# The start of a two-layer decoder trunk: two projections of the first layer made block by block, or together along the rows of the weights

## The chip, the core and the metric

The kernel runs on one core of a Trainium2 chip, as one launch. The metric is the device time of that launch in microseconds (us); a smaller time is better. In the views of the profile the engines are called PE (matrix multiply), PEld (its weight load), DVE (vector engine), ACT (scalar engine), POOL and SP. SP issues most of the DMAs here.

## What is computed

The reference is a decoder trunk of two layers on 256 tokens of width 1024, float32 throughout. Each layer has three token mixers side by side on one normalised input, and then a squared-ReLU MLP:

```python
def hybrid_mixer(h, w_in, ...):
    p = h @ w_in
    (cq, ckv, k_rope, mq, mk, mv, rq, rk, rv, rg, g_mla, g_moba, g_ret) = jnp.split(p, IN_SPLIT_IDX, axis=-1)
    o_mla = mla_branch(cq, ckv, k_rope, mla_q_norm, mla_kv_norm, mla_w_q_up, mla_w_kv_up, cos_mla, sin_mla)
    o_moba = moba_branch(mq, mk, mv, cos_moba, sin_moba)
    o_ret = retention_branch(rq, rk, rv, rg, ret_gn_w, ret_gn_b, cos_ret, sin_ret)
    merged = (jax.nn.sigmoid(g_mla) * (o_mla @ w_branch_mla)
              + jax.nn.sigmoid(g_moba) * (o_moba @ w_branch_moba)
              + jax.nn.sigmoid(g_ret) * (o_ret @ w_branch_ret))
    return merged @ w_out

for l in range(DEPTH):
    h = rms_norm(x, attn_norm[l])
    x = x + hybrid_mixer(h, w_in[l], ...)
    h = rms_norm(x, mlp_norm[l])
    x = x + squared_relu_mlp(h, w_mlp_up[l], w_mlp_down[l])
return rms_norm(x, final_norm)
```

The columns of `w_in` that matter here come first: 416 columns for the MLA branch (256 for the query's low rank, 128 for the key's and value's, 32 for the shared rotary key), then three times 512 for the MoBA branch's `mq`, `mk` and `mv`. In the MLA branch the 416 columns are normalised again, then widened by `mla_w_q_up` and `mla_w_kv_up` to queries, keys and values of 8 heads.

## The kernel before

**Numbers in two parts.** Every operand of a large product is split into a high part (`hi`, written by ACT in a shorter format) and the rest (`lo`, by DVE: raw minus high). A product is then three matmuls into the same bank (`three`, lines 209 to 212): high by high, high by low, low by high. `fetch` (line 181) does the split for weights: L190 on ACT writes `whi`, L191 on DVE writes `wlo`. `split` (L225 on ACT, L226 on DVE) does it for activations, with the norm's gain. The norm's own factor, one number per token, is applied when a product is copied out of its bank.

**Weights.** `weight_plan` lays all weights out in the order of use, one DMA per load. A load mostly holds two row tiles (128 rows each) of 512 columns, 512 KB. `load_w` fetches in that order, one load ahead of use, except for the very first block. There are 4 buffers for raw weights and 6 each for `whi` and `wlo`.

**The first block, called "b0".** It multiplies x by the 416 MLA columns. In layer 0 it comes in five loads: the row tiles 0 and 1 singly, then three pairs. After it comes the block "mq" (512 columns, four loads of two row tiles), then "mk", both made by `project` (line 316): for each row tile k of x, for each of the two token halves, `three`. All row tiles of one block are done before the next block begins. x itself comes in parts: the row tiles 0 and 1 singly, then 2 and 3, then 4 to 7. x once more by tokens (`xrow`, for the norm's sum of squares) and the constants `K` are asked for after the first seven weight loads and before the rest.

**Banks.** There are eight accumulation banks, four in a group "acc" and four in a group "misc". `b0`, `mq`, `mk` and `mv` take two of "acc" each; transposes, scores and small products take "misc". In `kvup` (line 632) the MLA keys and then the values (into `vml`, L639) also take "acc".

**Order.** The code is a list of units (`prog`) with steps hung on them (`at`). A planner reorders the instructions of all engines by its own forecast of their times, except inside `manual_schedule` regions, where the written order stands. Such a region covers ACT, DVE and PE during the first block of layer 0 (`first_x`, line 1008). On the chip each engine then works strictly through its own list. The steps that matter here: `c_norms` (L543 to L558), which copies the 416 columns out of their banks and normalises them, hangs on unit 1 of "mq"; `c_turn` (L591 to L601), which transposes them and splits them into `cTh` and `cTl`, hangs on unit 1 of "mk"; `qrope`, `qnope` and `kvup` widen them between the units of "mv"; then the attention heads begin (scores `ps_s`, L666). Before x arrives PE multiplies zeros eight times (`warm`, L507, the constant `WARM`).

Of the kernel before, what the change touches and what calls it, by code (L numbers as in the profile page):

```python
# [7 lines left out]
F32 = mybir.dt.float32  # L8
# [5 lines left out]
P = 128  # L14
D = 1024
S = 256
NT = S // P
# [25 lines left out]
C_KV = [P * h + o + i for o in (0, NOPE) for h in range(MLA_H) for i in range(64)]  # L43


def b0_units(l):


    return ((0, 1), (1, 1), (2, 2), (4, 2), (6, 2)) if l == 0 else ((0, 2), (2, 2), (4, 2), (6, 2))


def weight_plan():

    plan = []

    def block(key, name, kt, cols, per):
        for j in range(0, kt, per):
            plan.append(((*key, j // per), name, (j, per), cols))

    def span(c, n):  # L60
        return range(c, c + n)

    for l in range(L):
        for i, unit in enumerate(b0_units(l)):
            plan.append(((l, "b0", i), "w_in", unit, C_MLA))
        block((l, "mq"), "w_in", KD, C_MQ, 2)
        block((l, "mk"), "w_in", KD, C_MK, 2)
        block((l, "mv"), "w_in", KD, C_MV, 2)
        mv, plan = plan[-4:], plan[:-4]
        for i, (key, name, kt, cols) in enumerate(  # L70
            (("qrope", "mla_w_q_up", 2, C_QROPE), ("qnope", "mla_w_q_up", 2, C_QNOPE), ("kvup", "mla_w_kv_up", 1, C_KV))
        ):
            block((l, key), name, kt, cols, kt)
            plan.append(mv[i])
        plan.append(mv[3])
        for i in range(2):
            block((l, "gmla%d" % i), "w_in", KD, span(C_GMLA + 512 * i, 512), 2)
        for i in range(2):
            block((l, "gmoba%d" % i), "w_in", KD, span(C_GMOBA + 512 * i, 512), 2)
        for i in range(2):  # L80
            block((l, "bmla%d" % i), "w_branch_mla", 4, span(512 * i, 512), 2)
        block((l, "rqk"), "w_in", KD, C_RQK, 2)
        block((l, "rv"), "w_in", KD, C_RV, 2)
        for n in range(4):
            block((l, "rg", n), "w_in", KD, span(C_RG + P * n, P), KD)
        for i in range(2):
            block((l, "bmoba%d" % i), "w_branch_moba", 4, span(512 * i, 512), 2)
        for i in range(2):
            block((l, "gret%d" % i), "w_in", KD, span(C_GRET + 512 * i, 512), 2)
        for i in range(2):  # L90
            block((l, "bret%d" % i), "w_branch_ret", 4, span(512 * i, 512), 2)
        for n in range(KD):
            block((l, "wout", n), "w_out", KD, span(P * n, P), KD)
        for f in range(NF + LAG):
            if f < NF:
                block((l, "up", f), "w_mlp_up", KD, span(P * f, P), KD)
            if f >= LAG:
                plan.append(((l, "down", f - LAG, 0), "w_mlp_down", (f - LAG, 1), range(D)))
    at, offset = {}, 0
    for key, name, (j, n), cols in plan:  # L100
        at[key] = (offset, n, len(cols))
        offset += P * n * len(cols)
    return plan, at, offset
# [22 lines left out]
def trunk(ctx: ExitStack, tc: tile.TileContext, x, wts, consts, gains, gfin, xtok, out):  # L126
# [36 lines left out]

    def load_w(*key):

        ahead = 0 if key[:2] == (0, "b0") else AHEAD
        while order and len(loaded) < ahead + 1:
            first = order.pop(0)
            loaded[first] = fetch(first)
        return loaded.pop(key)  # L170
# [10 lines left out]
    def fetch(key):  # L181
        offset, n, c = where[key]
        sz = n * c
        raw = started.pop(key, None)
        if raw is None:
            raw = wp.tile([P, 1024], F32, name="raw", bufs=4)
            transfer(key, raw)
        hi = wp.tile([P, 1024], F32R, name="whi", bufs=6)
        lo = wp.tile([P, 1024], F32R, name="wlo", bufs=6)
        nc.scalar.activation(hi[:, :sz], raw[:, :sz], AF.Copy)  # L190
        nc.vector.tensor_sub(lo[:, :sz], raw[:, :sz], hi[:, :sz].bitcast(F32))  # L191
        return (
            hi[:, :sz].rearrange("p (k c) -> p k c", k=n),
            lo[:, :sz].rearrange("p (k c) -> p k c", k=n),
        )
# [120 lines left out]
    def project(l, key, xn, n, done=None, before=None, turns=(range(NT),)):  # L316

        accs, ws = [], []
        units = b0_units(l) if key == "b0" else [(j, 2) for j in range(0, KD, 2)]
        count = len(units)  # L320

        def unit(i, ts, j):
            if not accs:
                accs.extend(acc_tile() for _ in range(NT))
            if before:
                before(i)
            if len(ws) <= j:
                ws.append(load_w(l, key, j))
            wh, wl = ws[j]
            for kk in range(units[j][1]):  # L330
                k = units[j][0] + kk
                ah, al = xn.k(k)
                for t in ts:
                    sl = slice(P * t, P * t + P)
                    three(accs[t][:, :n], ah[:, sl], al[:, sl], wh[:, kk, :], wl[:, kk, :], k == 0, k == KD - 1)
            if i == count * len(turns) - 1:
                done(accs)

        for turn, ts in enumerate(turns):
            for j in range(count):  # L340
                i = turn * count + j
                prog.append(((key, i), lambda i=i, ts=ts, j=j: unit(i, ts, j)))
# [168 lines left out]
    def at(slot, step):  # L511
        steps.setdefault(slot, []).append(step)

    def slot(key, j):
        return [k for k, _ in prog].index((key, j))
# [9 lines left out]
    def layer(l, xn, before):  # L525
# [5 lines left out]

        def c_norms():
            accs = b0
            if l == 0:
                xn.stats_rows(xrows)
            else:
                for n in range(KD):
                    xn.square(n)
                xn.stats()
# [17 lines left out]
                    dst = krx[t][:, 64 * (1 - i) : 64 * (1 - i) + 64].rearrange("p (two n) -> p two n", two=2)  # L557
                    nc.vector.tensor_copy(dst[:, :, 16 * i : 16 * i + 16], kr[:, 0, :, :])  # L558

        project(l, "b0", xn, 416, b0.extend, before, ((0,), (1,)) if l else (range(NT),))  # L560


        def moba_done(key):
            def done(accs):
                dst = mqkv[key] = [w2k(key) for _ in range(NT)]
                for t in range(NT):
                    nc.scalar.activation(dst[t], accs[t], AF.Copy, scale=xn.col[t])
                    if key != "mv":
                        xv = dst[t].rearrange("p (h d) -> p h d", h=MB_H)[:, :, 0:16]
                        rope(xv.rearrange("p h (two n) -> p h two n", two=2), K_COS_MB, K_SIN_MB, t, 8, MB_H)  # L570

            return done

        project(l, "mq", xn, 512, moba_done("mq"))
        at(slot("mq", 1), c_norms)
        at(slot("mq", 2), xn.stats_row)
        project(l, "mk", xn, 512, moba_done("mk"))


# [20 lines left out]
            nc.vector.tensor_copy(KK[0:64, 1::2, :], krT[0:64, None, :].to_broadcast([64, 4, S]))  # L600
            nc.vector.tensor_copy(KK[64:P, 0::2, :], krT[64:P, None, :].to_broadcast([64, 4, S]))  # L601

        at(slot("mk", 1), c_turn)

        def nope(dst, w, ks, copy):
            for b in range(2):
# [25 lines left out]
        def kvup():  # L632
            wh, wl = load_w(l, "kvup", 0)
            nope(mla["K"], (wh[:, :, 0:512], wl[:, :, 0:512]), (2,), nc.vector.tensor_copy)
            for t in range(NT):
                acc = acc_tile()
                sl = slice(P * t, P * t + P)
                three(acc, c["h"][:, 2, sl], c["l"][:, 2, sl], wh[:, 0, 512:1024], wl[:, 0, 512:1024], True, True)
                nc.scalar.activation(mla["v"][t], acc, AF.Copy)  # L639
# [348 lines left out]
    xn = Normed(G_ATT)  # L988
    xrows = [w2k("xrow") for _ in range(2 * NT)]
    nc.sync.dma_start(chunk(0), x[:, 0, :])  # L990
    for i, (k, n) in enumerate(b0_units(0)):
        if k == 2:
            nc.sync.dma_start(X[0][:, 2:4, :], x[:, 2:4, :])
        elif k == 4:
            nc.sync.dma_start(X[1], x[:, 4:8, :])
        tag, bufs = ("t4", T4) if n == 2 else ("w2k", W2K)
        started[0, "b0", i] = sb.tile([P, 512 * n], F32, name="raw0", tag=tag, bufs=bufs)
        transfer((0, "b0", i), started[0, "b0", i])
    for i in range(2):
        started[0, "mq", i] = wp.tile([P, 1024], F32, name="raw", bufs=4)  # L1000
        transfer((0, "mq", i), started[0, "mq", i])
    for q in range(2 * NT):
        nc.sync.dma_start(xrows[q], xtok[:, q // 2, 512 * (q % 2) : 512 * (q % 2) + 512])
    nc.sync.dma_start(K, consts[:, :K_DEC])

    started_order = ExitStack()

    def first_x(i):
        if i == 0:
            started_order.enter_context(  # L1010
                tc.manual_schedule(engines={mybir.EngineType.Activation, mybir.EngineType.DVE, mybir.EngineType.PE})
            )
            at(slot("b0", len(b0_units(0)) - 1), started_order.close)
        k, n = b0_units(0)[i]
        for j in range(k, k + n):
            xn.take(j, False)

    before = first_x
    for l in range(L):
# [1 line left out]


W2K = 17
WARM = 8
ENDS = 4
FIRST = 3
WHOLE = 1
# [1 line left out]
T4 = 9  # L1029
# [76 lines left out]
```

## Time and profile before

| | us |
|---|---|
| median of 3 runs (lowest, highest) | 861.49 (861.37, 861.53) |
| the profiled execution, its own time | 861.24 |
| its span, from the first to the last instruction | 859.5 |
| PE busy, of the span | 849.2 |
| DVE busy, of the span | 618.1 |
| ACT busy, of the span | 507.7 |

The profiled execution's time is 1.74 us more than its span, and 0.25 us under the median of the runs. In the timeline a row gives start and length in us, then engine, line, operation, what it writes and reads, and in brackets the idle time before it with what ended it. Consecutive matmuls overlap, so the pace of PE is read from one start to the next, not from the lengths, and a busy share of 99% does not mean that PE never waited.

### The profile page before, as it was taken

How to read it: one execution, taken by the hardware profiler on the slowest of the kernel's cores; microseconds unless marked ns; L12 is line 12 of the kernel's file. 1: busy time of each engine (PE TensorE's matmuls, PEld its weight loads, DVE VectorE, ACT ScalarE, POOL GpSimd, SP SyncE). 2: the span in 40 equal slices, each digit the busy share in tenths (PEclk: the TensorE clock that was granted, in tenths of full speed). 3: DMA queues.
4: the chain of work that ended last, by engine and by line, in shares of the span. 5: the costliest groups of instructions: out<-in, count | busy, mean ns of one | idle time of the engine just before them, and what ended most of it. 6: DMA issues, size and time to landing. Idle time of an engine off the chain costs nothing.

```text
span 859.5 us, 12496 instructions
## 1 busy us (share of the span) xinstructions
PE 849.2 (99%) x4544; PEld 728.8 (85%) x4544; DVE 618.1 (72%) x1198; ACT 507.7 (59%) x885; POOL 12.1 (1%) x23
## 2 busy tenths in 40 slices
PE   8999999999999999999999999999999999999997
PEld 7888888988898888888888888889889988888885
DVE  6896787787777666666589767977877776666664
ACT  7766776535456555555577567665355565555553
POOL 0000000000000000000000000000100000000000
PEclk9999999999999999999999999999999999999999
DMA  9775344446366665555356455445565666666641
GB/s 339 235 233 172 124 147 140 148 155 194 126 196 195 202 192 192 183 188 192 109 202 213 153 159 163 139 140 168 150 194 148 174 205 191 190 182 185 196 123 50
DMA packets 42541, 150.08 MB, mean 175 GB/s; under 512 B 4848, under 2 KB 5360, under 8 KB 42480
## 3 DMA queue, kind: packets, MB, share of 16 engines
q1 hardware_dynamic: 42192, 149.13, 55.7%
q8 instruction: 36, 0.59, 0.3%
q10 hardware_dynamic: 288, 0.16, 0.1%
q14 instruction: 25, 0.20, 0.1%
HBM read 148.22 MB, written 1.05 MB: 174 GB/s over the span
## 4 chain that ended last, share of the span: by engine, by line
PE 96%; DVE 1%; ACT 1%; issue 1%; DMA 1%; SPq 0%; POOLq 0%; POOL 0%; ACTq 0%
PE acc L210 22%; PE acc L211 22%; PE acc L212 22%; PE pup L873 13%; PE pup L874 7%; PE po L428 2%; PE ps_s L666 1%; PE ps_pt L421 1%; PE ps_s L388 1%; PE po L429 1%; DMA raw<-wts 1%; ACT whi L190 0%; PE pqk L686 0%; DVE wlo L191 0%; PE ps_r L388 0%
## 5 line engine op out<-in xcount | busy, mean ns | idle before, releaser
L191 DVE TENSOR_TENSOR wlo<-raw,whi 128x1024 fp32r<-128x1024 f32 (+2 forms) x279 | 336.3, 1209 | 164.2 <-ACT whi L190 162.3
L190 ACT ACTIVATE whi<-raw 128x1024 fp32r<-128x1024 f32 (+2 forms) x279 | 292.0, 1048 | 257.7 <-PE acc L212 152.0
L873 PE MATMUL pup<-xs,whi 128*128 128x512 f32 x496 | 176.9, 398 | 0.0
L211 PE MATMUL acc<-wlo,xs 128*128 128x512 f32 (+1 forms) x384 | 151.8, 395 | 0.6 <-DVE wlo L191 0.6
L210 PE MATMUL acc<-whi,xs 128*128 128x512 f32 (+1 forms) x384 | 150.7, 397 | 0.4 <-ACT whi L190 0.3
L212 PE MATMUL acc<-whi,xs 128*128 128x512 f32 (+1 forms) x384 | 150.7, 393 | 0.0
L874 PE MATMUL pup<-xs,wlo 128*128 128x256 f32 x496 | 138.3, 280 | 0.0
L873 PEld LDWEIGHTS pup<-xs,whi 128*128 128x128 f32 x496 | 92.9, 188 | 21.3
L210 PE MATMUL acc<-whi,sq 128*128 128x512 f32 x256 | 101.5, 397 | 0.4 <-ACT sq L229 0.4
L211 PE MATMUL acc<-wlo,sq 128*128 128x512 f32 x256 | 100.0, 391 | 0.0
L212 PE MATMUL acc<-whi,sq 128*128 128x512 f32 x256 | 99.5, 393 | 0.0
L874 PEld LDWEIGHTS pup<-xs,wlo 128*128 128x128 f32 x496 | 93.6, 189 | 2.2
L210 PEld LDWEIGHTS acc<-whi,xs 128*128 128x128 f32 x384 | 72.2, 188 | 14.3 <-ACT whi L190 1.5
L211 PEld LDWEIGHTS acc<-wlo,xs 128*128 128x128 f32 x384 | 72.3, 188 | 14.1 <-DVE wlo L191 1.6
L212 PEld LDWEIGHTS acc<-whi,xs 128*128 128x128 f32 x384 | 72.3, 188 | 13.0
L212 PEld LDWEIGHTS acc<-whi,sq 128*128 128x128 f32 x256 | 47.9, 188 | 11.7 <-DVE sq L230 0.2
L210 PEld LDWEIGHTS acc<-whi,sq 128*128 128x128 f32 x256 | 48.0, 188 | 11.2 <-ACT sq L229 0.8
L211 PEld LDWEIGHTS acc<-wlo,sq 128*128 128x128 f32 x256 | 48.2, 188 | 8.8
L211 PE MATMUL acc<-mTl,whi 128*128 128x256 f32 x128 | 36.3, 284 | 1.0 <-DVE mTl L230 1.0
L210 PE MATMUL acc<-mTh,whi 128*128 128x256 f32 x128 | 36.2, 285 | 0.0
L212 PE MATMUL acc<-mTh,wlo 128*128 128x256 f32 x128 | 36.1, 283 | 0.0
L410 ACT ACTIVATE prob<-prob,smx 128x128 f32<-128x128 f32 x64 | 28.3, 445 | 7.5 <-DVE smx L407 7.2
(241 smaller groups left out, 1196.3 us busy)
## 6 DMA issues: line engine op xcount, KB each, us to landing
raw<-wts SPq DMA_DIRECT2D x268, 512.0 KB, 3.7
raw<-wts SPq DMA_DIRECT2D x7, 416.0 KB, 3.3
xrow<-xtok SPq DMA_DIRECT2D x4, 256.0 KB, 8.4
y<-y SPq DMA_DIRECT2D x4, 256.0 KB, 2.2
DEC<-consts SPq DMA_DIRECT2D x1, 768.0 KB, 7.5
x<-x SPq DMA_DIRECT2D x1, 512.0 KB, 6.3
raw<-wts SPq DMA_DIRECT2D x2, 256.0 KB, 3.7
gf<-gfin SPq DMA_DIRECT2D x1, 512.0 KB, 3.9
```

Source lines behind the costliest of these rows:

```text
L190: nc.scalar.activation(hi[:, :sz], raw[:, :sz], AF.Copy)
L191: nc.vector.tensor_sub(lo[:, :sz], raw[:, :sz], hi[:, :sz].bitcast(F32))
L210: nc.tensor.matmul(o, ah, bh, start=start, stop=False)
L211: nc.tensor.matmul(o, ah, bl, start=False, stop=False)
L212: nc.tensor.matmul(o, al, bh, start=False, stop=stop)
L388: nc.tensor.matmul(o, b if swap else a, a if swap else b, start=i == 0, stop=i == 1)
L410: nc.scalar.activation(p[:, a:b], p[:, a:b], AF.Exp, bias=m[:, 2 + i : 3 + i], scale=scale, accum_out=m[:, 4 + i : 5 + i])
L421: nc.tensor.transpose(pt[:, P * i : P * i + P], got["p"][:, src : src + P], ident)
L428: nc.tensor.matmul(dst, v[0], pT[:, 0:S], start=True, stop=False)
L429: nc.tensor.matmul(dst[:, P:S], v[1], pT[:, S : 3 * P], start=False, stop=True)
L873: nc.tensor.matmul(u, wh[:, k, :], xm.both(k), start=k == 0, stop=False)
L874: nc.tensor.matmul(u[:, 0:S], wl[:, k, :], xm.k(k)[0], start=False, stop=k == KD - 1)
```

## The change

In layer 0 the blocks "b0" and "mq" become one: for each row tile k of x, the 416 and the 512 columns are multiplied in one unit (`start`), four banks filling side by side. Row tile 0 still has two loads, of 416 and of 512 columns; the row tiles 1 to 7 have one load each of 928 columns (464 KB), split by ACT and by DVE in two parts. Inside a unit all products with `whi` come first, then those with `wlo`. All these loads are asked for at the start, together with the first load of "mk", and `xrow` and `K` come after the other weights of the block. The two banks of "b0" come from "misc" in layer 0. `c_norms` hangs on the last unit of the new block, and `c_turn` on unit 2 of "mk". In both layers the two banks for the MLA values in `kvup` come from "misc". `WARM` goes from 8 to 9. The sums that are formed are the same. Layer 1 keeps its separate blocks.

```diff
     for l in range(L):
-        for i, unit in enumerate(b0_units(l)):
-            plan.append(((l, "b0", i), "w_in", unit, C_MLA))
-        block((l, "mq"), "w_in", KD, C_MQ, 2)
+        if l == 0:
+            plan.append(((l, "b0", 0), "w_in", (0, 1), C_MLA))
+            plan.append(((l, "mq", 0), "w_in", (0, 1), C_MQ))
+            for k in range(1, KD):
+                plan.append(((l, "b0mq", k), "w_in", (k, 1), range(0, 928)))
+        else:
+            block((l, "b0"), "w_in", KD, C_MLA, 2)
+            block((l, "mq"), "w_in", KD, C_MQ, 2)
...
-        nc.scalar.activation(hi[:, :sz], raw[:, :sz], AF.Copy)
-        nc.vector.tensor_sub(lo[:, :sz], raw[:, :sz], hi[:, :sz].bitcast(F32))
+        parts = (slice(0, 416), slice(416, sz)) if key[1] == "b0mq" else (slice(0, sz),)
+        for cs in parts:
+            nc.scalar.activation(hi[:, cs], raw[:, cs], AF.Copy)
+        for cs in parts:
+            nc.vector.tensor_sub(lo[:, cs], raw[:, cs], hi[:, cs].bitcast(F32))
...
+        def start(k, mq):
+            if k == 0:
+                b0.extend(misc_tile("b0") for _ in range(NT))
+                mq.extend(acc_tile() for _ in range(NT))
+            before(k)
+            ah, al = xn.k(k)
+            w = None if k == 0 else load_w(l, "b0mq", k)
+            jobs = []
+            for accs, key, cs in ((b0, "b0", slice(0, 416)), (mq, "mq", slice(416, 928))):
+                if k == 0:
+                    w = load_w(l, key, 0)
+                    cs = slice(0, cs.stop - cs.start)
+                jobs += [(accs[t][:, : cs.stop - cs.start], slice(P * t, P * t + P), w, cs) for t in range(NT)]
+            for part in ("high", "low"):
+                for o, sl, w, cs in jobs:
+                    if part == "high":
+                        nc.tensor.matmul(o, ah[:, sl], w[0][:, 0, cs], start=k == 0, stop=False)
+                        nc.tensor.matmul(o, al[:, sl], w[0][:, 0, cs], start=False, stop=False)
+                    else:
+                        nc.tensor.matmul(o, ah[:, sl], w[1][:, 0, cs], start=False, stop=k == KD - 1)
+            if k == KD - 1:
+                moba_done("mq")(mq)
+
+        if l:
+            project(l, "mq", xn, 512, moba_done("mq"))
+            at(slot("mq", 1), c_norms)
+            at(slot("mq", 2), xn.stats_row)
+        else:
+            mq = []
+            for k in range(KD):
+                prog.append((("start", k), lambda k=k: start(k, mq)))
+            at(slot("start", KD - 2), lambda: xn.stats_rows(xrows))
+            at(slot("start", KD - 1), c_norms)
+            at(slot("start", KD - 1), xn.stats_row)
...
-        at(slot("mk", 1), c_turn)
+        at(slot("mk", 1 if l else 2), c_turn)
...
             for t in range(NT):
-                acc = acc_tile()
+                acc = misc_tile("pv")
...
+    begin((0, "b0", 0), "w2k", W2K)
+    begin((0, "mq", 0), "w2k", W2K)
+    begin((0, "b0mq", 1), "t4", T4)
+    nc.sync.dma_start(X[0][:, 2:4, :], x[:, 2:4, :])
+    begin((0, "b0mq", 2), "t4", T4)
+    begin((0, "b0mq", 3), "t4", T4)
+    nc.sync.dma_start(X[1], x[:, 4:8, :])
+    begin((0, "b0mq", 4), "t4", T4)
+    for k in range(5, KD):
+        begin((0, "b0mq", k))
     for q in range(2 * NT):
         nc.sync.dma_start(xrows[q], xtok[:, q // 2, 512 * (q % 2) : 512 * (q % 2) + 512])
+    begin((0, "mk", 0))
     nc.sync.dma_start(K, consts[:, :K_DEC])
...
-            at(slot("b0", len(b0_units(0)) - 1), started_order.close)
-        k, n = b0_units(0)[i]
-        for j in range(k, k + n):
-            xn.take(j, False)
+            at(slot("start", KD - 3), started_order.close)
+        xn.take(k, False)
...
-WARM = 8
+WARM = 9
```

More of the change, by code (lines that the diff above doesn't have):

```diff
@@ L43 @@
 C_KV = [P * h + o + i for o in (0, NOPE) for h in range(MLA_H) for i in range(64)]
-def b0_units(l):
-    return ((0, 1), (1, 1), (2, 2), (4, 2), (6, 2)) if l == 0 else ((0, 2), (2, 2), (4, 2), (6, 2))
 def weight_plan():
@@ L164, in load_w @@
     def load_w(*key):
-        ahead = 0 if key[:2] == (0, "b0") else AHEAD
+        ahead = 0 if key[:2] in ((0, "b0"), (0, "mq"), (0, "b0mq")) else AHEAD
         while order and len(loaded) < ahead + 1:
@@ L318, in project @@
         accs, ws = [], []
-        units = b0_units(l) if key == "b0" else [(j, 2) for j in range(0, KD, 2)]
-        count = len(units)
+        per = where[l, key, 0][1]
+        count = KD // per
         def unit(i, ts, j):
@@ L329, in unit @@
             wh, wl = ws[j]
-            for kk in range(units[j][1]):
-                k = units[j][0] + kk
+            for kk in range(per):
+                k = per * j + kk
                 ah, al = xn.k(k)
@@ L533, in c_norms @@
             accs = b0
-            if l == 0:
-                xn.stats_rows(xrows)
-            else:
+            if l:
                 for n in range(KD):
@@ L558, in c_norms @@
                     nc.vector.tensor_copy(dst[:, :, 16 * i : 16 * i + 16], kr[:, 0, :, :])
-        project(l, "b0", xn, 416, b0.extend, before, ((0,), (1,)) if l else (range(NT),))
+        if l:
+            project(l, "b0", xn, 416, b0.extend, before, ((0,), (1,)))
         def moba_done(key):
@@ L572, in moba_done @@
             return done
-        project(l, "mq", xn, 512, moba_done("mq"))
-        at(slot("mq", 1), c_norms)
-        at(slot("mq", 2), xn.stats_row)
+        def start(k, mq):
[20 more added lines that the diff above has]
+                moba_done("mq")(mq)
+        if l:
+            project(l, "mq", xn, 512, moba_done("mq"))
[8 more added lines that the diff above has]
+            at(slot("start", KD - 1), xn.stats_row)
         project(l, "mk", xn, 512, moba_done("mk"))
@@ L990, in trunk, with begin, first_x @@
     nc.sync.dma_start(chunk(0), x[:, 0, :])
[L991 to L1001, printed above, removed]
+    def begin(key, tag=None, bufs=None):
+        if tag:
+            started[key] = sb.tile([P, 512 if tag == "w2k" else 1024], F32, name="raw0", tag=tag, bufs=bufs)
+        else:
+            started[key] = wp.tile([P, 1024], F32, name="raw", bufs=4)
+        transfer(key, started[key])
+    begin((0, "b0", 0), "w2k", W2K)
[8 more added lines that the diff above has]
+        begin((0, "b0mq", k))
     for q in range(2 * NT):
         nc.sync.dma_start(xrows[q], xtok[:, q // 2, 512 * (q % 2) : 512 * (q % 2) + 512])
+    begin((0, "mk", 0))
     nc.sync.dma_start(K, consts[:, :K_DEC])
     started_order = ExitStack()
-    def first_x(i):
-        if i == 0:
+    def first_x(k):
+        if k == 0:
             started_order.enter_context(
```

## The prediction

> **What bounds the kernel now.** I read the page first, then PE's list of waits, then PE's timeline at the start.
>
> ```profile
> PE 849.2 (99%) x4544; PEld 728.8 (85%) x4544; DVE 618.1 (72%) x1198; ACT 507.7 (59%) x885; POOL 12.1 (1%) x23
> PE 96%; DVE 1%; ACT 1%; issue 1%; DMA 1%; SPq 0%; POOLq 0%; POOL 0%; ACTq 0%
> PE acc L211 <- DVE mTl L230: 1.0, 2, 0.5
> PE acc L210 <- ACT sq L229: 0.4, 1, 0.4
> ```
>
> PE carries 96% of the chain that ended last, and the change leaves the number and the widths of its products as they are (one warm-up matmul is added). So only time in which PE waits can be won. Beyond the start the list of waits has just these 1.4 us, at places that the change does not touch. The rest of PE's waiting is at the start. Its rows there (start, length; the pace is read from start to start):
>
> ```profile
> 1.42 3.78 PE L507 MATMUL warm<-zero 128*128 128x512 f32 x8 [1.42 <-DVE zero L152]
> 5.29 0.71 PE L210 MATMUL acc<-whi,xs 128*128 128x416 f32 x1
> 5.91 0.67 PE L211 MATMUL acc<-wlo,xs 128*128 128x416 f32 x1
> 6.42 0.36 PE L212 MATMUL acc<-whi,xs 128*128 128x416 f32 x1
> ...
> 8.12 0.34 PE L212 MATMUL acc<-whi,xs 128*128 128x416 f32 x1
> 8.81 0.46 PE L210 MATMUL acc<-whi,xs 128*128 128x416 f32 x1 [0.34 <-ACT whi L190]
> 9.87 0.46 PE L211 MATMUL acc<-wlo,xs 128*128 128x416 f32 x1 [0.60 <-DVE wlo L191]
> 10.16 0.35 PE L212 MATMUL acc<-whi,xs 128*128 128x416 f32 x1
> ...
> 11.29 0.35 PE L212 MATMUL acc<-whi,xs 128*128 128x416 f32 x1
> ...
> 12.05 0.35 PE L210 MATMUL acc<-whi,xs 128*128 128x416 f32 x1
> 12.41 0.46 PE L211 MATMUL acc<-wlo,xs 128*128 128x416 f32 x1
> 12.71 0.35 PE L212 MATMUL acc<-whi,xs 128*128 128x416 f32 x1
> ...
> 18.22 0.39 PE L210 MATMUL acc<-whi,xs 128*128 128x512 f32 x1
> ...
> 20.72 0.39 PE L212 MATMUL acc<-whi,xs 128*128 128x512 f32 x1
> ```
>
> From 10.16 to 11.29 lie six starts, 0.188 us each: the pace of 416 columns. From 18.22 to 20.72 lie eleven, 0.227 each: the pace of 512. What exceeds the pace is waiting: 5.29 to 6.42 holds two matmuls, 1.13 - 0.38 = 0.75; then 0.69 - 0.19 = 0.50 (to 8.81), 1.06 - 0.19 = 0.87 (to 9.87), 0.29 - 0.19 = 0.10, 0.36 - 0.19 = 0.17 (to 12.41), 0.30 - 0.19 = 0.11. The sum is **2.50 us**. The brackets name whi and wlo, but behind those stand the loads, as ACT's rows and the stretches of DMA show:
>
> ```profile
> 4.68 0.55 ACT L190 ACTIVATE whi<-raw 128x416 fp32r<-128x416 f32 x1 [0.50 <-DMA raw<-wts]
> 5.54 0.54 ACT L190 ACTIVATE whi<-raw 128x416 fp32r<-128x416 f32 x1
> 6.79 0.91 ACT L225 ACTIVATE xs<-x,G 128x256 fp32r<-128x256 f32 x2 [0.72 <-DMA x<-x]
> 7.86 0.90 ACT L190 ACTIVATE whi<-raw 128x832 fp32r<-128x832 f32 x1 [0.16 <-DMA raw<-wts]
> 9.36 0.91 ACT L225 ACTIVATE xs<-x,G 128x256 fp32r<-128x256 f32 x2 [0.60 <-DMA x<-x]
> 5.00:6.00 1.00, 0.92 (x3) 0.38 (x2) 0.73 (x2) 1.00 (x3) 0.00 (x0) 1.00 1.00 208
> 15.00:20.00 5.00, 5.00 (x25) 4.49 (x24) 2.50 (x10) 3.92 (x13) 0.71 (x1) 1.00 1.04 410
> ```
>
> The last column is GB/s. The DMA engines are full and each transfer is used as soon as it lands. Per row tile of x, PE has six matmuls of 416 columns, 6 x 0.188 = 1.13 us, for 208 KB of weights and 128 KB of x, which take 0.84 us at 410 GB/s and 1.65 at the 208 of the sixth microsecond. Early on the loads are the slower side.
>
> **The block itself.** In the new unit a row tile gives PE 6 x 0.188 + 6 x 0.227 = 2.49 us of work for 464 + 128 KB, 1.48 us at 410 GB/s. So PE becomes the slower side once two or three loads are in. I work out when. Up to a landing, the queue before brought: 363 KB by 4.68, 699 by 5.54, 955 by 6.79, 1371 by 7.86, 1883 by 9.36. In the new order the first 491 KB are the same; then come mq's first load (747 KB in all, about 5.8), row tile 1 (1211 KB, 7.45), x 2 and 3 (1467 KB, 8.15), row tile 2 (1931 KB, 9.5), row tile 3 (2395 KB, 10.65). The splits cost:
>
> ```profile
> L190 ACT ACTIVATE whi<-raw 128x512 fp32r<-128x512 f32 x1 | 0.6, 617 | 0.0
> L191 DVE TENSOR_TENSOR wlo<-raw,whi 128x416 fp32r<-128x416 f32 x2 | 1.2, 588 | 0.6 <-ACT whi L190 0.6
> L191 DVE TENSOR_TENSOR wlo<-raw,whi 128x512 fp32r<-128x512 f32 x1 | 0.7, 684 | 0.0
> ```
>
> Per row tile ACT has about 0.5 + 0.55 + 0.62 = 1.7 us and DVE 0.5 + 0.59 + 0.68 = 1.8, both under 2.49. So the splits keep up.
>
> In row tile 0, the high part of 416 columns is ready at 5.23 as before. The ninth warm-up matmul (3.78 / 8 = 0.47 each) holds PE until about 5.45. PE is slow here: a 128x512 warm-up matmul takes 0.47 against 0.227, and the first row at the usual pace starts at 6.42. The four high products of 416 columns, at 0.38 each until 6.42, end at about 6.75. mq's high part is ready at 5.8 + 0.62 = 6.42, its low part at 7.1: both hidden. From 6.75 PE has 8 x 2.49 - 0.75 = 19.17 us of work, so row tile 0 ends at 8.49. Row tile 1 needs its first high part then, and has it at 7.45 + 0.55 = 8.0; the second at 8.6, needed at 9.2. Row tile 2 has its own at 10.1, needed at 10.98, row tile 3 at 11.5, needed at 13.5. No further wait: the block ends at 25.92. Before, the same work ends at 5.29 + 19.92 + 2.50 = 27.71. **The gain is 1.79 us.** Its bounds: 2.09 if PE is fast from 5.45 on (then mq's high part at 6.45 decides); 1.3 if the loads land half a microsecond later than I interpolate. I take 1.79, nearest to the rows.
>
> **What is moved behind it.** The token copy of x and `K` stand behind 1.0 and 1.5 MB more of weights in SP's queue and, at 410 GB/s, land near 19.2 and 21.4; their first users, `c_norms` and the transposes of the norm's factor, now begin at 25.5. "mk"'s first load lands near 20.5 and is needed at 25.9; SP issues the next ones when DVE has freed the raw buffers of row tiles 5 to 7, which land at about 14.2, 15.4 and 16.6 and are split within 2 us. All hidden. "c" is later, however:
>
> ```profile
> 18.68 1.11 ACT L543 ACTIVATE c<-acc,ms 128x416 f32<-128x416 f32 x2 [1.08 <-POOL ms L295]
> 25.60 0.34 DVE L551 TENSOR_SCALAR c<-c,ssc 128x256 f32<-128x256 f32 x1
> 25.86 0.28 DVE L553 TENSOR_SCALAR c<-c,ssc 128x128 f32<-128x128 f32 x1
> 33.60 0.71 PE L591 MATMUL pct<-K,c 128*128 128x128 f32 x5
> 39.84 0.28 PE L210 MATMUL misc<-whi,cTh 128*128 128x256 f32 x1
> L360 DVE TENSOR_TENSOR ropea<-c,K 128x32 f32<-128x32 f32 x2 | 0.4, 187 | 0.5 <-ACT c L543 0.5
> 25.00:41.00 16.00, 13.17 (x24) 1.00 0.83 271
> 41.00:58.00 17.00, 16.18 (x31) 1.00 0.74 243
> ```
>
> The chain from L543 to the end of L553 took 7.46 us, at leisure beside weight splits. It now starts at 25.7 and would end at 33.2; `c_turn` stands behind three units of "mk", 25.92 + 3 x 2.73 = 34.1. Cover 0.9 us. From `c_turn` to the first product of `qrope` there were 6.24 us, which "mk" filled. Now one unit of "mk" and, if the planner puts it there, one of "mv" fill 0.7 + 2 x 2.73 = 6.2. I take nothing lost; the cover is thin, and a rival below prices it.
>
> **The values' banks.**
>
> ```profile
> 57.09 0.69 DVE L616 COPY KK<-acc 64x512 f32<-64x512 f32 x1
> 58.78 0.58 PE L210 MATMUL acc<-whi,cTh 128*128 128x512 f32 x1
> 59.20 0.40 PE L211 MATMUL acc<-wlo,cTh 128*128 128x512 f32 x1
> ```
>
> The second value product starts only behind the key copies that free its bank; with banks of "misc" it can go earlier. PE was not idle there: other work stood before it, and its pace is 0.42 - 0.23 = 0.19 off. So between -0.2 and +0.2 us in each layer; I take 0, since PE had work.
>
> **The sum.** 861.24 (the profiled execution) - 1.79 = 859.45. That execution lay 0.25 under the median of the runs, so **859.7** there. A measurement of this kernel can tell about 0.2%, 1.7 us, from no change; the forecast stands just beyond that. Its own range is 859.0 to 860.2.
>
> **Rivals.**
>
> *DVE becomes the bound behind the block* (13%). For: from 41 to 58 DVE was busy 16.18 of 17. `c_norms` has 20 DVE instructions, four long (2 x 0.62 us) and 16 of at most 0.187, at most 4.3 us; all but 0.6 ran before 26 and now run after. DVE was idle 2.83 us from 25 to 41 and 0.82 from 41 to 58, together 3.65. It would need 3.7, and 1.8 more since PE comes earlier: 1.85 too much. Against: "mk"'s splits can run ahead of PE, six deep. Price 0.8 to 1.8: 860.5 to 861.5.
>
> *PE stays slow beyond 6.42* (12%). Before, the waits of 0.50 and 0.87 us from 8.12 on would have hidden a later rise, so the close runs do not tell against it. Now PE has work throughout, and each microsecond at half pace costs half. At the far end, row tile 0 wholly at half pace, the remaining 1.74 us of it cost another 1.74. Middle 0.9: 860.6, between 860.2 and 861.4. [...]
>
> *`qrope` waits for c* (20%), slower. Place: PE's list is strict, and `qrope`'s products stand in it. If the planner leaves them right behind "mk", PE arrives at 34.1 + 0.7 + 2.73 = 37.5 and cTl, 6.24 behind `c_turn`, at 40.3: 2.8 lost. If the c chain runs 1.5 us beyond its cover, since mq's copies (1.2 us) now share ACT with it, `c_turn` also waits: 4.3 in all. 859.7 + 2.8 = 862.5, 859.7 + 4.3 = 864.0, and 865 if DVE adds to it. It decides when cTl comes later than PE's fill, and it is slower beyond 0.2% from a wait of 3.5 us on (15 of the 20). For: cTl was made by a DVE at 95%. Against: "mv" units are there to fill, and before no wait arose.
>
> *More than forecast* (6%): PE fast from 5.45, and 0.2 won at the values in each layer, 2.09 + 0.4: 859.0 or a little less.
>
> **How the numbers follow.** The forecast has 49%, of which 34 lie beyond 0.2% and 15 within. With the last case, faster is 0.34 + 0.06 = 0.40; within 0.2% is 0.15 + 0.13 + 0.12 + 0.05 of `qrope`'s mild end = 0.45; slower is 0.15. The range 858.9 to 861.6 holds the forecast, both middle rivals and part of the last: about 0.8.
>
> **What would show it.** Right: PE's starts 0.188 and 0.227 apart from about 6.7 on, no gap above 0.3 us from 8 to 26, the first "mk" product at about 26. L543 near 25.7, `pct` near 34, the `misc` products of `qrope` near 38 to 40 with no idle PE before. Wrong: gaps at row tile 1 (loads late); starts 0.38 or 0.45 apart beyond 7 (slow PE); a wait of PE for cTl or c (`qrope`); PE waiting for wlo between 40 and 60 (DVE).

## The result, and the profile after

| | us |
|---|---|
| before, median of 10 runs (lowest, highest) | 861.62 (861.37, 862.92) |
| after, median of 10 runs (lowest, highest) | 859.44 (858.82, 859.85) |
| after / before | 0.9972, 95% interval 0.9963 to 0.9982 |
| the profiled execution after, its own time | 859.10, 2.14 under that of before (span 857.3) |

The changed kernel is faster by 0.28% (0.18 to 0.37), 2.2 us between the medians. The forecast was 859.7.

PE's timeline at the start of the changed kernel (start, length, engine, line, what it writes and reads). L594 and L595 are the products with `whi`, L597 those with `wlo`; `b` is a bank of 416 columns, `acc` one of 512:

```profile
1.43 4.00 PE L510 MATMUL warm<-zero 128*128 128x512 f32 x9 [1.43 <-DVE zero L152]
5.26 0.40 PE L594 MATMUL b<-whi,xs 128*128 128x416 f32 x1
5.50 0.35 PE L595 MATMUL b<-whi,xs 128*128 128x416 f32 x1
5.69 0.35 PE L594 MATMUL b<-whi,xs 128*128 128x416 f32 x1
5.88 0.34 PE L595 MATMUL b<-whi,xs 128*128 128x416 f32 x1
6.13 0.50 PE L594 MATMUL acc<-whi,xs 128*128 128x512 f32 x1
6.46 0.40 PE L595 MATMUL acc<-whi,xs 128*128 128x512 f32 x1
...
7.99 0.35 PE L594 MATMUL b<-whi,xs 128*128 128x416 f32 x1
...
10.04 0.63 PE L597 MATMUL acc<-wlo,xs 128*128 128x512 f32 x2
10.60 0.45 PE L594 MATMUL b<-whi,xs 128*128 128x416 f32 x1
10.89 0.35 PE L595 MATMUL b<-whi,xs 128*128 128x416 f32 x1
...
25.82 0.38 PE L316 MATMUL pss<-K,ms 128*128 128x128 f32 x2
```

Read from start to start, with 0.19 for 416 columns and 0.23 for 512: 5.26 to 5.50 has 0.05 too much, 5.88 to 6.13 has 0.06, 6.13 to 6.46 has 0.10. Of the pair at 10.04 the second starts at 10.28; to 10.60 that is 0.09 too much, and 10.60 to 10.89 is 0.10. That is 0.4 us of waiting in place of 2.50. The last row, the transposes of the norm's factor right behind the block, marks its end.

What was left of the waits is again the loads. ACT's rows, with what ended its idle time:

```profile
7.02 1.07 ACT L192 ACTIVATE whi<-raw 128x416 fp32r<-128x416 f32 x2 [0.55 <-DMA raw<-wts]
8.82 0.51 ACT L228 ACTIVATE xs<-x,G 128x256 fp32r<-128x256 f32 x1 [0.72 <-DMA x<-x]
10.00 1.07 ACT L192 ACTIVATE whi<-raw 128x416 fp32r<-128x416 f32 x2 [0.67 <-DMA raw<-wts]
```

Row tile 1 landed at 7.0 and was in use from 7.99, without a wait. Row tile 2 landed at 10.0, 0.55 us of split later PE could go on: that is the wait at 10.60.

PE's list of waits (engine and line, what it waited for: us in total, times, longest) has lost its two rows for whi and wlo and gained none:

```profile
PE warm L510 <- DVE zero L152: 1.4, 1, 1.4
PE acc L214 <- DVE mTl L233: 1.0, 2, 0.5
PE acc L213 <- ACT sq L232: 0.4, 1, 0.4
```

And the "c" chain, from its first step on ACT to the first product of `qrope`:

```profile
30.55 0.60 ACT L544 ACTIVATE c<-b,ms 128x416 f32<-128x416 f32 x1
38.76 0.82 PE L626 MATMUL pct<-K,c 128*128 128x128 f32 x6
43.76 0.28 PE L213 MATMUL misc<-whi,cTh 128*128 128x256 f32 x1
41.00:58.00 17.00, 15.82 (x28) 1.00 0.78 255
```

It is much later than before (18.68, 33.60, 39.84), yet PE waits for nothing in it: the planner put the whole of "mk" and 26 of the 48 products of "mv" ahead of `qrope`. The last row is DVE's busy time from 41 to 58 us, 15.82 of 17, a little less than the 16.18 of before.

### The profile page after: what moved, and what is told of

It reads as the page before. It is cut to its first block, busy times and chain, and to the rows that moved or that the text cites. A ratio compares the mean times of both kernels' runs of the same rounds, so it can differ in the third digit from the quotient of the medians.

```text
span 857.3 us, 12509 instructions
## 1 busy us (share of the span) xinstructions
PE 848.1 (99%) x4545; PEld 729.4 (85%) x4545; DVE 618.8 (72%) x1205; ACT 507.3 (59%) x892; POOL 12.1 (1%) x23
## 4 chain that ended last, share of the span: by engine, by line
PE 97%; DVE 1%; issue 1%; ACT 1%; POOL 0%; POOLq 0%; ACTq 0%
PE acc L213 21%; PE acc L214 21%; PE acc L215 21%; PE pup L908 13%; PE pup L909 7%; PE po L431 2%; PE ps_s L701 1%; PE ps_pt L424 1%; PE ps_s L391 1%; PE po L432 1%; PE warm L510 0%; PE acc L594 0%; PE acc L595 0%; PE acc L597 0%; PE pqk L721 0%
## 5 line engine op out<-in xcount | busy, mean ns | idle before, releaser
L194 DVE TENSOR_TENSOR wlo<-raw,whi 128x1024 fp32r<-128x1024 f32 (+3 forms) x286 | 336.8, 1184 | 157.1 <-ACT whi L192 156.6
L192 ACT ACTIVATE whi<-raw 128x1024 fp32r<-128x1024 f32 (+3 forms) x286 | 292.5, 1027 | 254.8 <-PE acc L215 152.2
L214 PE MATMUL acc<-wlo,xs 128*128 128x512 f32 (+1 forms) x352 | 139.3, 396 | 0.0
L213 PE MATMUL acc<-whi,xs 128*128 128x512 f32 (+1 forms) x352 | 138.9, 396 | 0.0
L215 PE MATMUL acc<-whi,xs 128*128 128x512 f32 (+1 forms) x352 | 138.2, 394 | 0.0
L215 PEld LDWEIGHTS acc<-whi,xs 128*128 128x128 f32 x352 | 66.2, 188 | 12.6
L213 PEld LDWEIGHTS acc<-whi,xs 128*128 128x128 f32 x352 | 66.1, 188 | 12.3
L214 PEld LDWEIGHTS acc<-wlo,xs 128*128 128x128 f32 x352 | 66.2, 188 | 12.1
```

The source lines that it names most:

```text
L192: nc.scalar.activation(hi[:, cs], raw[:, cs], AF.Copy)
L194: nc.vector.tensor_sub(lo[:, cs], raw[:, cs], hi[:, cs].bitcast(F32))
L213: nc.tensor.matmul(o, ah, bh, start=start, stop=False)
L214: nc.tensor.matmul(o, ah, bl, start=False, stop=False)
L215: nc.tensor.matmul(o, al, bh, start=False, stop=stop)
```

## The experiments

All ran beside the kernel before. The times to hold them against are 861.6 to 861.7 for before and 859.44 for the changed kernel.

**The block alone.** The changed kernel without its other three edits:

```diff
-                acc = misc_tile("pv")
+                acc = acc_tile()
-        at(slot("mk", 1 if l else 2), c_turn)
+        at(slot("mk", 1), c_turn)
-WARM = 9
+WARM = 8
```

> The changed kernel with the block and its loads alone: the values' banks back in acc, WARM 8, c_turn on unit 1 of mk. Theory (the whole gain is PE's waiting for loads at the start): 859.3 to 859.7, the 2.2 us under the kernel before all but kept, and PE's waits from 5 to 26 us again about 0.5 us in sum. Rival (the banks, the ninth warm-up matmul or the place of c_turn carry part of it): 860.0 or more, with a wait of PE in the trace that the changed kernel does not have, behind 26 us for banks and c_turn, before 6.5 us for the warm-up.

Measured: 861.47, ratio 0.9999 (0.9990 to 1.0008). The whole gain is gone, and the first theory with it. The start is nearly as short as in the changed kernel (the block ends at 25.92, after 25.82), but two new rows stand in PE's list of waits, both near 56 us (a third, 0.3 us for whi, is PE's idle time before its first product at 5.46):

```profile
PE acc L213 <- ACT vml L674: 0.7, 1, 0.7
PE acc L213 <- DVE KK L651: 0.5, 1, 0.5
```

**The banks alone**, in the kernel before:

```diff
-                acc = acc_tile()
+                acc = misc_tile("pv")
```

> The kernel before with the values' banks from misc, in both layers, and nothing else. Theory: within 0.3 us of the kernel before, 861.3 to 861.9, since PE had other work there. Rival (the banks give part of the gain): 861.2 or less.

Measured: 861.74, ratio 1.0001 (0.9992 to 1.0010). By themselves the banks are worth nothing, as forecast.

**The changed kernel with the values back in acc**, and nothing else:

```diff
-                acc = misc_tile("pv")
+                acc = acc_tile()
```

> The changed kernel with the values' two banks back in acc, and nothing else. First theory (only the start counts): 859.2 to 859.8. New theory, after the block alone gave nothing: the block makes c late, the planner spends the units of mv as filler ahead of qrope, and kvup then stands without other work and waits for its acc banks: 860.9 to 861.6, with PE's waits for KK and vml near 55 to 58 us, 1.5 to 2 us in sum, and the start as short as in the changed kernel. If instead the place of c_turn or the warm-up did it in the earlier run, this one stays below 859.9 and has no such wait.

Measured: 861.33, ratio 0.9995 (0.9986 to 1.0004), 1.9 us over the changed kernel. The block ends at 25.77. PE's timeline in `kvup`:

```profile
54.60 0.49 PE L680 MATMUL pqr<-K,qr 128*128 128x128 f32 x3
55.61 0.47 PE L213 MATMUL acc<-whi,cTh 128*128 128x512 f32 x1 [0.53 <-DVE KK L651]
...
56.15 0.40 PE L215 MATMUL acc<-whi,cTl 128*128 128x512 f32 x1
57.24 0.50 PE L213 MATMUL acc<-whi,cTh 128*128 128x512 f32 x1 [0.69 <-ACT vml L674]
57.57 0.40 PE L214 MATMUL acc<-wlo,cTh 128*128 128x512 f32 x1
57.81 0.39 PE L215 MATMUL acc<-whi,cTl 128*128 128x512 f32 x1
58.29 0.47 PE L213 MATMUL acc<-whi,xs 128*128 128x512 f32 x1
```

The first value product waits until the key copies have freed a bank, the second until the first has been copied out of it (56.15 to 57.24 holds one matmul: 0.86 too much), and the next one 0.25. In the changed kernel the same products run earlier, without a wait:

```profile
52.44 0.47 PE L213 MATMUL pv<-whi,cTh 128*128 128x512 f32 x1
...
53.93 0.39 PE L213 MATMUL pv<-whi,cTh 128*128 128x512 f32 x1
```

So the two edits hold each other up: the block wins 2 us at the start, and without the banks they are given back at 55 to 58. Why the bank is missed only with the block, the timelines suggest. Before, `qrope` began at 39.84, right after "mk", so all 48 products of "mv" came behind it, and the last 15 of them stood between the keys and the first value product (56.97):

```profile
53.56 0.40 PE L210 MATMUL acc<-whi,xs 128*128 128x512 f32 x1
...
56.74 0.39 PE L212 MATMUL acc<-whi,xs 128*128 128x512 f32 x1
56.97 0.39 PE L210 MATMUL acc<-whi,cTh 128*128 128x512 f32 x1
```

With the block "c" is late, 26 products of "mv" are spent ahead of `qrope`, and the other 22 are done by 52.93, ahead of the last key products. In the run with the values in acc only the three small products of 54.60 stand between the keys and the values. The order is read from the rows; that it is the lateness of "c" which brings it about, no run isolates.

**The place of c_turn**, put back to unit 1 of "mk":

```diff
-        at(slot("mk", 1 if l else 2), c_turn)
+        at(slot("mk", 1), c_turn)
```

> The changed kernel with c_turn hung on unit 1 of mk in both layers, as before. New theory (banks decide, the planner places c_turn by its own forecast): within 0.3 us of the changed kernel, 859.1 to 859.7, c_turn's transposes again near 38 us. Rival (the slot is what keeps the gain): 860.5 or more, with PE waiting for c or cTl between 28 and 45 us.

Measured: 859.49, ratio 0.9971 (0.9960 to 0.9983). Nothing depends on it, the planner puts the transposes where it did:

```profile
38.78 0.82 PE L626 MATMUL pct<-K,c 128*128 128x128 f32 x6
```

**Eight warm-up matmuls** in the changed kernel (`WARM = 8`):

> The changed kernel with 8 warm-up matmuls as before. The ninth fills the time until the first weights are split, so without it PE starts no earlier (5.26 us) and idles 0.2 to 0.4 us before. Theory: within 0.2 us of the changed kernel if the clock rises by then anyway; up to 0.5 us slower if the rise comes later without it (859.4 to 860.0). Rival (its forecast effect on the planner matters as in the run of the block alone): 861 or more.

Measured: 859.25, ratio 0.9970 (0.9958 to 0.9981): no difference by the median. Its profiled execution, however, took 859.81, and shows PE at half pace far into the first row tile (PE began 0.15 us sooner, at 5.11, and not at 5.26 as expected):

```profile
5.11 0.71 PE L594 MATMUL b<-whi,xs 128*128 128x416 f32 x1
5.62 0.55 PE L595 MATMUL b<-whi,xs 128*128 128x416 f32 x1
5.97 0.55 PE L594 MATMUL b<-whi,xs 128*128 128x416 f32 x1
6.32 0.55 PE L595 MATMUL b<-whi,xs 128*128 128x416 f32 x1
6.67 0.63 PE L594 MATMUL acc<-whi,xs 128*128 128x512 f32 x1
7.09 0.55 PE L595 MATMUL acc<-whi,xs 128*128 128x512 f32 x1
7.48 0.40 PE L594 MATMUL acc<-whi,xs 128*128 128x512 f32 x1
7.71 0.40 PE L595 MATMUL acc<-whi,xs 128*128 128x512 f32 x1
```

Starts 0.35 apart at 416 columns (0.19 in the changed kernel's profile) and the usual 0.23 at 512 columns only from 7.48 on. The block ends at 26.43 in place of 25.82. The trace also holds a record of the clock granted to PE, which the views do not print: the full clock is granted from 7.41 us on in this execution, and from 5.09 in that of the changed kernel.

**Who sets the pace: six more warm-up matmuls**, in the kernel before (`WARM = 14`) and in the changed one (`WARM = 15`).

> The kernel before with 14 warm-up matmuls in place of 8, so that PE begins its first block some 1.5 to 2 us later. Theory (loads set the pace of the start): the time stays within 0.3 us of the kernel before, 861.3 to 861.9; the waits at 8.8 and 9.9 us shrink or go, the one for the low part of the third load stays. Rival (PE's own early start or early clock sets it, and the changed kernel gained by its earlier clock): 1.3 us or more slower, 862.9 or more.

> The changed kernel with 15 warm-up matmuls in place of 9, the same six more as in the other kernel of this pair. Theory (behind the first row tile PE and not the loads sets the pace): the delay shows, less the 0.4 us of waits it covers: 1.0 to 1.6 us over the changed kernel, 860.4 to 861.0. Rival (loads still set the pace of the new block): no more than 0.3 us over the changed kernel, 859.7 or less. With PE's clock risen before the first product, its runs should lie closer together than the 1.0 us of the changed kernel's ten runs if the moment of the rise is what spreads those.

Measured: 861.72 for before with 14, ratio 1.0000 (0.9991 to 1.0009), and 862.07 for the changed kernel with 15. In the first, PE begins 1.0 us later (6.29 in place of 5.29), and 17 us on, the transposes of the norm's factor come 0.1 later (22.41, after 22.30):

```profile
1.42 5.02 PE L507 MATMUL warm<-zero 128*128 128x512 f32 x14 [1.42 <-DVE zero L152]
6.29 0.35 PE L210 MATMUL acc<-whi,xs 128*128 128x416 f32 x1
...
8.86 0.46 PE L210 MATMUL acc<-whi,xs 128*128 128x416 f32 x1 [0.15 <-ACT whi L190]
9.92 0.45 PE L211 MATMUL acc<-wlo,xs 128*128 128x416 f32 x1 [0.60 <-DVE wlo L191]
...
22.41 0.38 PE L313 MATMUL pss<-K,ms 128*128 128x128 f32 x2
```

and the last of these rows in the kernel before:

```profile
22.30 0.38 PE L313 MATMUL pss<-K,ms 128*128 128x128 f32 x2
```

The loads set the old pace: a microsecond of PE is free there. In the changed kernel PE begins 1.43 us later (6.70) and the block ends 1.04 later (26.86): PE sets the new pace. That is as expected for the block. The time as a whole is not: it lies 1.1 us above the expected range. The planner's order behind the block is another, and 1.9 us more are lost there (last column of the table below). Longer or new waits for `mv` near 58 us and for `mTl` and `th` near 222 to 226 are 0.8 of them by the list of waits; where the rest is lost was not followed up. The runs lie 1.4 us apart, not closer, so the spread of the changed kernel's runs was not shown to come from PE's early pace.

**Splits in one piece:**

```diff
-        parts = (slice(0, 416), slice(416, sz)) if key[1] == "b0mq" else (slice(0, sz),)
+        parts = (slice(0, sz),)
```

> The changed kernel with each load of 928 columns split in one piece on ACT and on DVE. ACT then gives the high part of 928 columns about 1.0 us after landing, in place of 0.55 for the first 416. Theory: row tile 1 (landed at 7.0, needed at 7.99) gets its own at 8.0, no wait; row tile 2 (landed at 9.97, in use from 10.60) waits 0.4 us more: 859.7 to 860.0. If splits as a whole are cheaper (fewer instructions) and this shows: 859.4 or less. Rival (splits are hidden by the loads in both): 859.2 to 859.6.

Measured: 859.74, ratio 0.9973 (0.9962 to 0.9984). By the median 0.3 more, as expected; but the profiled execution also has a slow PE until 6.41 us, and its waits at the row tiles 1 and 2 are about 0.3 us in sum, so the splits' share is not settled.

**Products bank by bank** inside a unit:

```diff
-            for part in ("high", "low"):
-                for o, sl, w, cs in jobs:
+            for o, sl, w, cs in jobs:
+                for part in ("high", "low"):
```

> The changed kernel with the products of a unit bank by bank (high, high, low for each bank, as in the blocks of before) in place of all products with whi first. Theory: the low part of the first 416 columns is then needed 0.4 us after the first high product, and DVE has it 0.6 us after the high part, so PE waits some 0.2 us in each of the row tiles 0, 1 and 2: 0.4 to 0.6 us in sum, 859.8 to 860.1. Rival (the order within a unit does not matter, the landing alone counts): 859.2 to 859.6.

Measured: 859.30, ratio 0.9973 (0.9963 to 0.9984). The expectation missed: only row tile 2 waits (0.25 us, about what it waited anyway). Having all high products first is worth nothing.

**Two loads per row tile, another order of x, and both.**

```diff
-        nc.sync.dma_start(
-            raw[:, :sz], bass.AP(tensor=wts.tensor, offset=wts.offset + offset, ap=[[sz, P], [1, sz]])
-        )
+        for a, b in ((0, 416), (416, sz)) if key[1] == "b0mq" else ((0, sz),):
+            nc.sync.dma_start(
+                raw[:, a:b], bass.AP(tensor=wts.tensor, offset=wts.offset + offset + a, ap=[[sz, P], [1, b - a]])
+            )
```

```diff
-    nc.scalar.dma_start(X[0][:, 1, :], x[:, 1, :])
...
     begin((0, "mq", 0), "w2k", W2K)
+    nc.sync.dma_start(chunk(1), x[:, 1, :])
     begin((0, "b0mq", 1), "t4", T4)
-    nc.sync.dma_start(X[0][:, 2:4, :], x[:, 2:4, :])
+    nc.sync.dma_start(chunk(2), x[:, 2, :])
     begin((0, "b0mq", 2), "t4", T4)
+    nc.sync.dma_start(chunk(3), x[:, 3, :])
     begin((0, "b0mq", 3), "t4", T4)
```

> The changed kernel with each row of 928 weight columns fetched by two DMAs, of 416 and of 512 columns, into the same buffer. Theory (what counts is PE's work per byte, not the width of a load): no slower, 859.0 to 859.6; PE's wait at row tile 2 (0.2 us) goes, since its first 416 columns land some 0.5 us sooner. Rival (wide loads carry part of the gain, or SP's eight DMAs in flight bind with twice as many): 859.9 or more, with waits at row tiles 2 to 5.

> The changed kernel with row tile 1 of x asked for on SP behind mq's first load, and the row tiles 2 and 3 of x singly, each ahead of its weights. Theory: the first weights land about 0.2 us sooner and mq's about 0.3, PE's first product at 5.0 to 5.1, and the waits of 0.2 us before mq's first product and of 0.2 at row tile 2 go: 0.3 to 0.5 us under the changed kernel, 858.9 to 859.2, as far as the moment of the clock's rise lets it show. Rival (already hidden, or x then comes late): 859.4 or more.

> Both of the last two together. Theory: no wait of PE above 0.1 us from its first product to the end of the block, 858.8 to 859.2. Rival: the waits were hidden behind the slow clock anyway, 859.3 or more.

Measured: 859.81 (ratio 0.9977, 0.9968 to 0.9985), 859.73 (0.9979, 0.9970 to 0.9987) and 859.96 (0.9978, 0.9969 to 0.9987). None beats the changed kernel, and the theory missed in all three. The wait at row tile 2 did go in all three profiles; here with two loads, where L598 is the product with `wlo` and the pair's second starts at 11.05:

```profile
10.81 0.63 PE L598 MATMUL acc<-wlo,xs 128*128 128x512 f32 x2
11.28 0.35 PE L595 MATMUL b<-whi,xs 128*128 128x416 f32 x1
11.46 0.35 PE L596 MATMUL b<-whi,xs 128*128 128x416 f32 x1
```

But PE gets its full pace only from 6.76 us on with two loads and from 7.31 in the new order of x (5.09 in the changed kernel), and that cost more than the 0.2 us of the wait. In the first, the first weights also landed 0.4 us later (ACT's first split begins at 5.02, after 4.60). In the second they landed sooner (4.13), yet PE was still busy with its nine slow warm-up matmuls and began at 5.43. So these profiles do not tell what the edits are worth by themselves, and why the medians lie 0.3 to 0.5 us over the changed kernel stays open. With both edits, PE waits about 0.25 us inside row tile 1 (before 9.16), and later for the "c" chain at `c_turn`, at 39.7 us:

```profile
PE pct L626 <- DVE c L552: 0.7, 2, 0.4
```

**All profiles together.** The end of the block is the start of the norm's transposes; "rest" is the execution's own time less that; "full clock" is the moment from which the trace records PE's full clock as granted.

| kernel | full clock | PE's first product | row tile 1 begins | block ends | own time | rest |
|---|---|---|---|---|---|---|
| changed kernel | 5.09 | 5.26 | 7.99 | 25.82 | 859.10 | 833.28 |
| c_turn on unit 1 | 4.42 | 5.17 | 8.17 | 25.83 | 859.14 | 833.31 |
| bank by bank | 5.50 | 5.43 | 8.05 | 25.96 | 859.30 | 833.34 |
| two loads | 6.76 | 5.62 | 8.76 | 26.40 | 859.78 | 833.38 |
| splits in one piece | 6.41 | 5.42 | 8.54 | 26.41 | 859.74 | 833.33 |
| 8 warm-up matmuls | 7.41 | 5.11 | 8.79 | 26.43 | 859.81 | 833.38 |
| order of x | 7.31 | 5.43 | 8.81 | 26.46 | 859.77 | 833.31 |
| both load edits | 5.87 | 5.42 | 8.15 | 26.17 | 860.52 | 834.35 |
| 15 warm-up matmuls | 5.33 | 6.70 | 9.22 | 26.86 | 862.07 | 835.21 |
| values in acc | 5.68 | 5.42 | 8.13 | 25.77 | 861.17 | 835.40 |
| block alone | 5.55 | 5.46 | 8.13 | 25.92 | 861.40 | 835.48 |

In seven kernels the rest is the same within 0.1 us: whatever happens at the start reaches the end one to one. The other four each have a wait of their own behind the block: for "c", in the planner's other order, and twice for the banks. Where the full clock comes by 5.7 us, the block ends between 25.77 and 25.96 (15 warm-up matmuls aside); in the four rows where it comes at 6.4 or later, between 26.40 and 26.46, whatever the edit.

## Why the prediction was right, and where not

**What binds the start: right.** The loads set the old pace (a later PE costs 0.1 of 1.0 us), PE the new one (1.04 of 1.43), and the 2.5 us of waits shrank to 0.4.

**The size: 1.79 forecast, 2.1 in the trace** (2.50 - 0.40 + 0.03 for the earlier first product; 2.14 between the profiled executions). The term that was off is row tile 0, where PE was taken at half pace until 6.42, as in the profile of before. In the profile after, it ran at full pace from 5.50 (starts at 5.50, 5.69 and 5.88, 0.19 apart), and row tile 0 ended 0.5 us sooner than forecast (7.99 for 8.49). The gain then equals the upper bound given for that case, 2.09, in part by chance: that bound had PE wait for mq's high part until 6.45, but its products began at 6.13, and row tile 2 took 0.2 back. The early rise of the clock was not forecast: it came at 5.09 here, the third earliest of the 14 profiles (4.42 to 7.41), and at 6.40 in the profile of before. The landings were out by up to 0.7 us (row tile 1 at 7.0 for 7.45, x 2 and 3 at 8.8 for 8.15, row tile 2 at 10.0 for 9.5), which cost 0.2 us at row tile 2 where none was forecast.

**PE slow for longer: a rival that is real.** It did not strike the profile after, but it did in four others: row tile 0, 2.49 us of work, took 3.68 with 8 warm-up matmuls and 3.38 in the new order of x, 0.95 and 0.65 more than the 2.73 of the changed kernel. No run shows the 0.9 taken for its middle: by the end of the block its price is 0.6 us (26.40 to 26.46 in the four, after 25.82). The latest rise of the clock in the 14 profiles was at 7.41.

**The values' banks: the step that failed.** They were costed at nothing, plus or minus 0.2, since PE had other work beside them. That holds for the kernel before (0.1 us, within its interval), but with the block they carry 1.9 us. The prediction took the cover from the old timeline and then moved that cover away itself: it let "mv" fill the time before `qrope`, without asking what would then be left beside `kvup`. It was 26 products of "mv", a little over two units, in place of the one unit that it counted. That the number came out in spite of this is luck: the change held the banks as well, and the same sum would give the block alone about 859.7 too, which measured 861.47.

**`qrope` waits for c: not there, but near.** The chain began at 30.55 and not 25.7, `c_turn` stood at 38.76 and not 34.1: the planner gave way twice over, and PE did not wait. With both load edits it did, 0.7 us, which the thin cover had led one to expect.

**DVE as the bound: no.** From 41 to 58 it was busy 15.82 of 17, less than before and not more than there is room for, and PE's list of waits has no wait for wlo.

## What to carry to other kernels

When loads set the pace at the start, give PE more work per byte that has landed: here a row of weights for two blocks at once, with which PE's waits went from 2.50 to 0.4 us. Then look where the work was that used to lie between the steps moved, since a cover taken for one stall is missing at the next; and test the edits of a change in pairs, because one that is worth nothing alone can hold the whole gain.

## What the runs showed of the hardware

PE's early slow pace (0.35 from start to start at 416 columns, after it 0.19) does not end at a fixed time. With the first warm-up matmul at 1.42 to 1.43 in both, and two programs that differ up to there by one warm-up matmul, full pace was reached by 5.5 us in one execution (`c_turn` on unit 1: starts at 5.47, 5.65 and 5.84, 0.19 apart) and only between 7.1 and 7.5 in another (8 warm-up matmuls, rows above). The record of the granted clock in the traces says the same: the full clock begins at 4.42 us in the first and at 7.41 in the second, the earliest and the latest of all 14 profiles. (The clock column of the views reads 1.00 there in both, since the record begins only with that moment.) The record of the full clock lasts 846.51, 849.92 or 853.33 us in the 14 profiles, steps of 3.41 us; what makes the steps no run shows. In the order-of-x run, where the full clock begins at 7.31, the starts tell it row by row, 0.35 apart at 416 columns up to 6.82, then 0.43, 0.27 and 0.23 at 512:

```profile
6.47 0.55 PE L594 MATMUL b<-whi,xs 128*128 128x416 f32 x1
6.82 0.62 PE L593 MATMUL acc<-whi,xs 128*128 128x512 f32 x1
7.25 0.43 PE L594 MATMUL acc<-whi,xs 128*128 128x512 f32 x1
7.52 0.40 PE L593 MATMUL acc<-whi,xs 128*128 128x512 f32 x1
7.75 0.39 PE L594 MATMUL acc<-whi,xs 128*128 128x512 f32 x1
```

In the one execution the full clock came 3.0 us after the first matmul, in the other 6.0; what decides the moment no run shows. The old kernel had waits for loads at 8.81 and 9.87 that could hide a late rise; its profiles show full pace from 6.42 on, from 6.30 on with the banks from misc, and from its first product at 6.29 on with 14 warm-up matmuls. In the new kernel a late rise costs up to 0.6 us by the end of the block (26.46 in the order-of-x run, after 25.82), and an edit worth 0.2 us at the start cannot be told from it by one profile.
